# Queries and keys of the fourth retention head: two blocks of eight-step sums replaced by one quad of seven half-token products

## The chip, the cores and the metric

The kernel runs on one core of a Trainium2 chip. The core has a matrix engine (TensorE, shown as PE; its weight loads are shown apart as PEld), three engines for elementwise work (VectorE, DVE; ScalarE, ACT; GpSimd, POOL), a sync engine whose queue issues transfers (SP), and 16 DMA engines that move data between the core's memory SBUF and the outer memory HBM. TensorE writes only to PSUM, a small memory of eight banks, from which the other engines take the sums. The metric is the device time of one execution in microseconds (us). The kernel before takes 1007.98 us, the median of three runs from 1007.86 to 1008.79.

## The reference

One layer of a bidirectional encoder, on 512 tokens of 1024 features, in float32. Cut to what matters here:

```python
h = rmsnorm(x, g_mix)
proj = h @ w_in                # columns: conv x, conv B, conv C, q, k, v, swish gate, gate A, gate R
qf = rotary(q by heads) * (256 ** -0.5)
kf = rotary(k by heads)        # 4 heads of 256 features
def rotary(t):
    t1, t2 = t[..., :128], t[..., 128:]
    return concatenate([t1 * cos - t2 * sin, t1 * sin + t2 * cos])
ret = retention over the tokens, forwards and backwards, of qf, kf, v
y_r = (groupnorm(ret) * g_ret * silu(g_sw)) @ w_r_out
x = x + (sigmoid(gate_a) * y_a + sigmoid(gate_r) * y_r) @ w_o     # y_a: the short convolution
x = x + (silu(h2 @ w_ff_gate) * (h2 @ w_ff_up)) @ w_ff_down
return rmsnorm(x, g_final)
```

The change touches `h @ w_in` for the 256 columns of q and the 256 columns of k of one head, and the rotary turn of these.

## The kernel before

Every float32 operand of a product is written as a sum of two parts in the format that TensorE takes at full rate: `split` (lines 213 to 224) lets ACT make the rounded part (line 216) and DVE the remainder (line 217). A product then takes three matmuls: high by high, high by low, low by high.

Most of the products are done as quads: two groups of weight columns and two halves of the tokens are taken as a two by two block product, with seven block products in place of eight (the Winograd form of Strassen's scheme). The sums of activations are made once (`sums`, line 715). The sums of weights are made as the weights are used: `prefetch_form` (line 311) adds two tiles of 128 by 1024 on DVE (line 322) for the forms t1 to t4, and splits the outcome into a pair of tiles whi and wlo from a pool of five pairs. The forms come in the order b11, t1, t2, b21, t3, t4, b22. A tile pair is called a unit here.

There are two ways to do a quad. `strassen` (line 469) gives sums with the tokens in the partitions. Its units serve 12 matmuls of 512 columns each, a form has two units, and a quad has 14 units and 168 matmuls. `fm_quad` (line 418) gives sums with the features in the partitions. A form is one unit there, and serves 24 matmuls of 256 columns (`prod`, line 407); a quad has 7 units and 168 matmuls. It keeps three banks: a and d are each added into several times, b once. Between the products ACT copies the sums so far out of bank a (`snap`, line 464: p1, u2 and u3), and DVE makes the four outcomes, each a tile of 128 by 512: the two halves of its columns are the two blocks of 128 features, at 256 tokens. They are handed to four functions: ev11 (after the fourth product), ev22 (after the fifth), ev21 (after the sixth; it gets bank a itself) and ev12 (after the seventh).

The third way, `feature_major` (line 383), does without sums of weights. It takes a block of 256 weight columns, two units in all, and for each of the two groups of 128 features it adds up eight steps of three matmuls of 512 columns (`mm3`, line 373). `do_qk` uses it twice for the fourth head, once for q and once for k.

The turn of q and k is `rotate` (line 755): for each of two outcomes, two multiplications by the tables of cosine and sine and one addition or subtraction on DVE, then `keep` (line 664), which splits the outcome (one ACT cast, one DVE subtraction) and stores both parts in HBM through the POOL queue. Each of these uses four tiles t of 128 by 512 (a, b, and the two parts), from a pool of nine that all snaps and sums use as well. The first three heads (EARLY = 3) have their sums early, and are turned later, one turn (of q or of k) behind each of the quads that follow (`turn_one`, line 770, called at ev21 of `do_quad`).

The main part runs in this order: sums of q and k of the first three heads; four quads of v and the swish gate (called v0 to v3 below), the fourth followed by `do_qk(3)`; two quads of the gates A and R (g0, g1); then `mix_quads` (line 887) with three `fm_quad` (x0, x1, x2) for the convolution; then retention and the rest. Loads of weights are listed in `plan` and `loads`, and go through the SP queue up to four entries of the plan ahead (LEAD), into ten raw tiles. Units are prepared at least two ahead (AHEAD). A planner sets the order of the instructions on each engine before the launch, from the order of the program, from which tiles are free, and from its own costs. On the chip each engine takes its instructions in that fixed order.

The names used for units below: g0.4 is the fifth unit of quad g0, counted from 0.

Of the kernel before, what the change touches and what calls it, by code (L numbers as in the profile page):

```python
# [13 lines left out]
F32R = mybir.dt.float32r  # L14
# [5 lines left out]
S = 512  # L20
# [3 lines left out]
QK = 256  # L24
# [5 lines left out]
C_XC, C_GB, C_GC, C_Q, C_K, C_V, C_G, C_GA, C_GR = (  # L30
    0, 1024, 2048, 3072, 4096, 5120, 7168, 9216, 10240)
# [24 lines left out]
FORMS = ("b11", "t1", "t2", "b21", "t3", "t4", "b22")  # L56
# [7 lines left out]
def plan():  # L64

    out = []

    def a(name, col):
        out.append(("c", name, 0, 8, col, 256))

    def b(name, row, nk, col, nc):
        out.append(("c", name, row, nk, col, nc))

    def quad(c0, c1):
        for name in FORMS:  # L80
            for u in (0, 2):
                out.append(("q", ("w", c0, c1), name, u, 2))

    for h in range(EARLY):
        for r in (0, 512):
            b("w_in", r, 4, (C_Q + h * QK, C_K + h * QK), 512)
    for h in range(HEADS):
        quad(C_V + h * VD, C_G + h * VD)
        if h >= EARLY:
            a("w_in", C_Q + h * QK)  # L90
            a("w_in", C_K + h * QK)
    for c in (0, 512):
        quad(C_GA + c, C_GR + c)
    for c0, c1 in ((C_XC, C_GC), (C_XC + 256, C_GC + 256), (C_GB, C_GB + 256)):
        for name in FORMS:
            out.append(("q", ("x", c0, c1), name, 0, 4))
    for s in (2, 3):
        for c in (C_XC, C_GC, C_GB):
            a("w_in", c + s * 256)
    def r(*names):  # L100
        for name in names:
            for u in (0, 2):
                out.append(("q", ("r",), name, u, 2))

    r("b11", "b21")
    out.extend(("q", ("p", 2, c), "b11", u, 2) for c in (0, 1) for u in (0, 2))
    r("t1", "t2", "t3", "b22")
    out.extend(("q", ("p", 3, 1), "b11", u, 2) for u in (0, 2))
    r("t4")
    out.extend(("q", ("p", 3, 0), "b11", u, 2) for u in (0, 2))  # L110
    for kind, name in [("a", x) for x in FORMS[:6]] + [("o", "b11"), ("a", "b22")] + [
            ("o", x) for x in ("t1", "t2", "b21", "b22", "t3", "t4")]:
        for u in (0, 2):
            out.append(("q", (kind,), name, u, 2))
    def f(q, *names):
        for n in names:
            if q == LONE:
                out.append(("q", ("f", q), n, 0, 4))
            else:
                for u in (0, 2):  # L120
                    out.append(("q", ("g", q), n, u, 2))

    def d(q0, n):
        names = FORMS if q0 + n == NQ else EARLY_FORMS
        units = [(name, u) for name in names for u in range(0, n, 2)]
        if q0 + n == NQ:

            i = units.index(("b21", 2))
            units[i:i + 3] = units[i + 1:i + 3] + units[i:i + 1]
        for name, u in units:  # L130
            out.append(("q", ("d", q0), name, u, min(2, n - u)))

    f(0, "b11", "b21")
    f(1, "b11")
    f(0, "t2", "t1", "t3", "t4", "b22")
    f(1, "t1", "t2", "b21", "t3", "t4", "b22")
    f(2, *FORMS)
    d(*FF_PARTS[0])
    f(3, *FORMS)
    f(4, *FORMS)  # L140
    d(*FF_PARTS[1])
    f(LONE, *FORMS)
    d(*FF_PARTS[2])
    return out
# [39 lines left out]
def block_kernel(ctx: ExitStack, tc: tile.TileContext, xw0, xw, xT, xtok, wpack, wquad, cols, decs, gret_rows, rot, g_ffn, g_final, out):  # L184
# [18 lines left out]
    def t512(dt=F32):  # L203
        return tmp.tile([P, 512], dt, tag="t512", name="t512")
# [178 lines left out]
    def feature_major(rhs, evict, block0=0):  # L383

        c = Chunk()
        for m in range(2):
            ps = bank()
            for k in range(8):
                mm3(ps, c.w(k, m * P, P), act_pair(rhs, k), k == 0, k == 7)
            evict(block0 + m, ps)  # L390
# [27 lines left out]
    def fm_quad(forms, ev11, ev21, ev22, ev12):  # L418

        def w():  # L420
            return take()[1][0]
        a, d, b = bank(), bank(), bank()
        prod(w(), forms["a11"], a, True)
        p1 = snap(a)
        prod(w(), forms["s1"], d, True)
        prod(w(), forms["s2"], a, False)
        u2 = snap(a)
        prod(w(), forms["a12"], b, True)
        nc.vector.tensor_tensor(out=p1, in0=b, in1=p1, op=ALU.add)
        ev11(p1)  # L430
        prod(w(), forms["s3"], a, False)
        u3 = snap(a)
        nc.vector.tensor_tensor(out=u3, in0=d, in1=u3, op=ALU.subtract)
        ev22(u3)
        prod(w(), forms["a22"], a, False)
        ev21(a)
        prod(w(), forms["s4"], d, False)
        nc.vector.tensor_tensor(out=u2, in0=d, in1=u2, op=ALU.subtract)
        ev12(u2)
# [133 lines left out]
    rcs = misctile(D, "rcs").rearrange("p (i n) -> p i n", i=2)  # L573
# [81 lines left out]
    qkd = [(kept(f"qh{h}"), kept(f"ql{h}")) for h in range(HEADS)]  # L655
# [6 lines left out]
          for j, n in enumerate((2, 2, 2, 1))]  # L662

    def keep(dst, src):
        hi, lo = t512(F32R), t512(F32R)
        split(src, hi, lo)
        for d, t in zip(dst, (hi, lo)):
            store(d, t.bitcast(F32))
# [83 lines left out]

    nc.vector.tensor_scalar_mul(lgam[:, 4:8], lgam[:, 4:8], -1.0)

    def rotate(h, j, t1, t2, table):
        cos, sin = table[:, 0, :], table[:, 1, :]
        for i, (c1, c2, op) in enumerate(((cos, sin, ALU.subtract), (sin, cos, ALU.add))):
            a, b = t512(), t512()
            nc.vector.tensor_tensor(out=a, in0=t1, in1=c1, op=ALU.mult)
            nc.vector.tensor_tensor(out=b, in0=t2, in1=c2, op=ALU.mult)  # L760
            nc.vector.tensor_tensor(out=a, in0=a, in1=b, op=op)
            keep([t[:, 2 * j + i, :] for t in qkd[h]], a)


    rcn = misctile(D, "rcn").rearrange("p (i n) -> p i n", i=2)
# [8 lines left out]
            rotate(h, j, early[h][:, 2 * j, :], early[h][:, 2 * j + 1, :], rcn)  # L774

    def do_qk(h):
        for j in range(2):
            pss = []
            feature_major(xg, lambda m, ps: pss.append(ps))
            rotate(h, j, *pss, rcs)  # L780


    def do_quad(left, right, func, func_left=None):
        def ev_sum(dst, o, f):
# [396 lines left out]
    def turn(half, th):  # L1181
        name = f"a{th + 1}{half + 1}"
        if not m32:
            t = [bigtile(), bigtile()]
            for j in range(4):
                m32[f"a{j // 2 + 1}{j % 2 + 1}"] = t[j // 2][:, j % 2 * 2:j % 2 * 2 + 2, :].rearrange(
                    "p a (b c) -> p (a b) c", c=256)
        if name != "a21":
            M[name] = form_tile()
        for tt in range(2):  # L1190
            ps = bank()
            for k in range(4):
                nc.tensor.transpose(ps[:, k * P:(k + 1) * P], sga[half][:, 2 * th + tt, k * P:(k + 1) * P], ident)  # L1193
            ps = ps.rearrange("p (k t) -> p k t", k=4)
            sl = slice(tt * P, (tt + 1) * P)
            if name != "a21":
                split(ps, *(t[:, :, sl] for t in M[name]))
            nc.scalar.copy(m32[name][:, :, sl], ps)
# [509 lines left out]
```

## Time and profile before

| what | value |
|---|---|
| median of three runs | 1007.98 us |
| the profiled execution | 1007.38 us, its span 1005.6 us |
| granted TensorE clock | 0.998 |
| PE busy | 995.0 us, 99% |
| DVE busy | 879.2 us, 87% |
| ACT busy | 558.0 us, 55% |
| POOL busy | 161.0 us, 16% |
| the chain that ended last | PE 96%, DVE 3% |

The span is the time from the first to the last instruction of the profiled execution; 1.8 us of its own time lie around it. Busy time is time in which an engine has an instruction of the program under way. Groups are listed by line of the code, engine and operation, with out<-in by the names of the tiles and their shapes. A line can be that of a helper: all splits stand at lines 216 and 217. "A <- B" in a list of waits reads: A waited for B.

### The profile page before, as it was taken

The page shows a single profiled execution, that of the slowest core. Times are in us where ns is not written, and L with a number is a line of the kernel's source. Part 1 is how long each engine was busy: PE and PEld are TensorE (multiplying, and loading weights), DVE is VectorE, ACT ScalarE, POOL GpSimd, SP SyncE. Part 2 cuts the span into 40 slices and gives each one's busy share as a digit, 9 for nine tenths or more (in the row PEclk, how much of TensorE's full clock was granted, in tenths as well). Part 3 has the DMA queues.
Part 4 walks back from the last instruction along what each step waited for, and adds up shares of the span by engine and source line. Part 5 has one row for each costly group of instructions (what it writes and reads, how often), then busy time and mean ns, then how long its engine had stood idle before and what let it go on. Part 6 is the DMA issues. An engine that isn't in the chain of part 4 may idle for free.

```text
span 1005.6 us, 13416 instructions
## 1 busy us (share of the span) xinstructions
PE 995.0 (99%) x4722; PEld 833.4 (83%) x4722; DVE 879.2 (87%) x1145; ACT 558.0 (55%) x751; POOL 161.0 (16%) x256
## 2 busy tenths in 40 slices
PE   9999999999999999999999999999999999999996
PEld 7888888888888998888888888888888888888885
DVE  7878888979798888977897797999988996989897
ACT  7547655563666454433455435577665555574665
POOL 0030221222122004122222110011101000003202
PEclk9999999999999999999999999999999999999999
DMA  9625587695767658899799995467677369487943
GB/s 355 198 76 182 185 287 221 206 306 175 228 196 248 218 224 297 323 321 270 210 246 242 407 308 185 134 211 223 167 229 179 115 213 268 107 249 130 272 143 105
DMA packets 65795, 222.70 MB, mean 221 GB/s; under 512 B 10240, under 2 KB 10368, under 8 KB 61632
## 3 DMA queue, kind: packets, MB, share of 16 engines
q1 hardware_dynamic: 46816, 149.46, 43.8%
q0 software_dynamic: 18624, 72.10, 27.2%
q8 instruction: 37, 0.61, 0.3%
q10 hardware_dynamic: 288, 0.29, 0.1%
q14 instruction: 30, 0.25, 0.1%
HBM read 173.83 MB, written 57.41 MB: 230 GB/s over the span
## 4 chain that ended last, share of the span: by engine, by line
PE 96%; DVE 3%; issue 0%; ACT 0%; POOL 0%; POOLq 0%; DVEq 0%; ACTq 0%
PE bank L459 61%; PE bank L415 8%; PE bank L375 7%; PE bank L376 7%; PE bank L377 7%; PE bank L401 4%; DVE wlo L217 1%; DVE raw L322 0%; PE bank L515 0%; PE bank L1247 0%; PE bank L1193 0%; DVE big L1550 0%; PE bank L700 0%; DVE big L1573 0%; DVE big L217 0%
## 5 line engine op out<-in xcount | busy, mean ns | idle before, releaser
L216 ACT CAST whi<-raw 128x1024 fp32r<-128x1024 f32 (+2 forms) x305 | 308.2, 1029 | 217.3 <-PE bank L459 77.9
L217 DVE TENSOR_TENSOR wlo<-raw,whi 128x1024 fp32r<-128x1024 f32 (+2 forms) x306 | 358.7, 1193 | 76.6 <-ACT whi L216 76.2
L459 PE MATMUL bank<-whi,xform 128*128 128x512 f32 x1056 | 330.5, 390 | 0.0
L459 PEld LDWEIGHTS bank<-whi,xform 128*128 128x128 f32 x1056 | 198.0, 188 | 42.2 <-DVE xform L217 1.1
L459 PE MATMUL bank<-whi,big 128*128 128x512 f32 x708 | 222.4, 389 | 0.2 <-ACT big L1544 0.2
L459 PE MATMUL bank<-wlo,xform 128*128 128x512 f32 x528 | 205.7, 389 | 0.0
L459 PEld LDWEIGHTS bank<-whi,big 128*128 128x128 f32 x708 | 132.9, 188 | 28.5 <-ACT big L1544 0.7
L322 DVE TENSOR_TENSOR raw<-raw 128x1024 f32<-128x1024 f32 x116 | 137.3, 1204 | 0.8
L459 PE MATMUL bank<-wlo,big 128*128 128x512 f32 x354 | 137.9, 390 | 0.0
L459 PEld LDWEIGHTS bank<-wlo,xform 128*128 128x128 f32 x528 | 99.1, 188 | 21.1 <-DVE wlo L217 0.7
L466 ACT COPY t<-bank 128x512 f32<-128x512 f32 x97 | 56.7, 587 | 78.4 <-PE bank L459 61.5
L375 PE MATMUL bank<-big,whi 128*128 128x512 f32 x220 | 85.7, 390 | 0.0
L377 PE MATMUL bank<-big,wlo 128*128 128x512 f32 x220 | 85.6, 389 | 0.0
L376 PE MATMUL bank<-big,whi 128*128 128x512 f32 x220 | 85.6, 389 | 0.0
L459 PEld LDWEIGHTS bank<-wlo,big 128*128 128x128 f32 x354 | 66.5, 188 | 13.9 <-DVE wlo L217 0.3
L415 PE MATMUL bank<-xform,whi 128*128 128x256 f32 x304 | 55.2, 283 | 0.0
L336 POOL DMA_DIRECT2D raw<-wquad x20 | 17.5, 877 | 217.9 <-ACT t L466 66.4
L377 PEld LDWEIGHTS bank<-big,wlo 128*128 128x128 f32 x220 | 41.3, 188 | 8.6
L376 PEld LDWEIGHTS bank<-big,whi 128*128 128x128 f32 x220 | 41.3, 188 | 8.6
L375 PEld LDWEIGHTS bank<-big,whi 128*128 128x128 f32 x220 | 41.3, 188 | 8.5
L415 PEld LDWEIGHTS bank<-xform,whi 128*128 128x128 f32 x304 | 47.5, 192 | 0.3 <-ACT t L466 0.2
L415 PE MATMUL bank<-xform,wlo 128*128 128x256 f32 x152 | 43.0, 283 | 0.0
(218 smaller groups left out, 1300.8 us busy)
## 6 DMA issues: line engine op xcount, KB each, us to landing
raw<-wquad SPq DMA_DIRECT2D x156, 512.0 KB, 5.1
raw<-wpack SPq DMA_DIRECT2D x26, 512.0 KB, 6.0
raw<-wquad POOLq DMA_DIRECT2D x20, 512.0 KB, 6.6
big<-turned SPq DMA_DIRECT2D x112, 64.0 KB, 4.2
t_g<-wquad POOLq DMA_DIRECT2D x12, 512.0 KB, 7.5
z<-t POOLq DMA_DIRECT2D x24, 256.0 KB, 4.6
t_o<-wquad POOLq DMA_DIRECT2D x12, 512.0 KB, 7.8
zform<-z POOLq DMA_DIRECT2D x6, 1024.0 KB, 12.9
```

Source lines behind the costliest of these rows:

```text
L216: first = (round or nc.scalar.copy)(hi, src)
L217: low_of[0] = nc.vector.tensor_tensor(out=lo, in0=src, in1=hi.bitcast(F32), op=ALU.subtract)
L322: nc.vector.tensor_tensor(out=t, in0=t, in1=raws[quad, more, u][:, 0:n], op=ALU.add)
L336: nc.gpsimd.dma_start(out=t[:, 0:n], in_=src[:, 0:n], accum_op=ALU.add)
L375: nc.tensor.matmul(ps, lh, rh, start=first, stop=False)
L376: nc.tensor.matmul(ps, lh, rl, start=False, stop=False)
L377: nc.tensor.matmul(ps, ll, rh, start=False, stop=last)
L401: nc.tensor.matmul(pss[tt], l, r, start=start and kk == 0 and i == 0, stop=stop and kk == 3 and i == 2, skip_group_check=True)
L415: nc.tensor.matmul(o, l[:, c], r[:, k], start=start and s == 0 and k == 0 and i == 0, stop=stop and k == 3 and i == 2, skip_group_check=True)
L459: nc.tensor.matmul(pss[tt], l, r[:, c], start=start and k == 0 and i == 0, stop=stop and k == n - 1 and i == 2, skip_group_check=True)
L466: nc.scalar.copy(t, ps)
```

## The change

The two blocks of q and k of the fourth head are taken out of the list of blocks and put into the plan as seven forms of an `fm_quad`, with q as the first group of columns and k as the second. `do_qk` makes one `fm_quad` in place of two calls of `feature_major`. Its four outcomes are q at the first 256 tokens, q at the last 256, k at the last 256 and k at the first 256; each is turned by itself, with 256 columns of the tables, and stored as half rows. `rotate` and `keep` get a slice of the tokens for this; for the other heads they do as before.

```diff
@@ -87,8 +87,8 @@
     for h in range(HEADS):
         quad(C_V + h * VD, C_G + h * VD)
         if h >= EARLY:
-            a("w_in", C_Q + h * QK)
-            a("w_in", C_K + h * QK)
+            for name in FORMS:
+                out.append(("q", ("x", C_Q + h * QK, C_K + h * QK), name, 0, 4))
     for c in (0, 512):
         quad(C_GA + c, C_GR + c)
@@ -662,7 +662,7 @@
     def keep(dst, src):
-        hi, lo = t512(F32R), t512(F32R)
+        hi, lo = (t512(F32R)[:, 0:src.shape[1]] for _ in range(2))
         split(src, hi, lo)
         for d, t in zip(dst, (hi, lo)):
             store(d, t.bitcast(F32))
@@ -752,14 +752,14 @@
-    def rotate(h, j, t1, t2, table):
-        cos, sin = table[:, 0, :], table[:, 1, :]
+    def rotate(h, j, t1, t2, table, sl=slice(0, S)):
+        cos, sin = table[:, 0, sl], table[:, 1, sl]
         for i, (c1, c2, op) in enumerate(((cos, sin, ALU.subtract), (sin, cos, ALU.add))):
-            a, b = t512(), t512()
+            a, b = (t512()[:, 0:sl.stop - sl.start] for _ in range(2))
             nc.vector.tensor_tensor(out=a, in0=t1, in1=c1, op=ALU.mult)
             nc.vector.tensor_tensor(out=b, in0=t2, in1=c2, op=ALU.mult)
             nc.vector.tensor_tensor(out=a, in0=a, in1=b, op=op)
-            keep([t[:, 2 * j + i, :] for t in qkd[h]], a)
+            keep([t[:, 2 * j + i, sl] for t in qkd[h]], a)
@@ -774,11 +774,9 @@
     def do_qk(h):
-        for j in range(2):
-            pss = []
-            feature_major(xg, lambda m, ps: pss.append(ps))
-            rotate(h, j, *pss, rcs)
-
+        def turn(j, half):
+            return lambda t: rotate(h, j, t[:, 0:256], t[:, 256:512], rcs, slice(256 * half, 256 * half + 256))
+        fm_quad(xf, turn(0, 0), turn(0, 1), turn(1, 1), turn(1, 0))
```

## The prediction

> **What bounds the kernel now.** I read the page's busy times first, then the chain of waits, then the busy time of each engine in the stretches around the change, and last the order of the instructions on DVE, ACT and PE there.
>
> ```profile
> span 1005.6 us, 13416 instructions
> ...
> PE 995.0 (99%) x4722; PEld 833.4 (83%) x4722; DVE 879.2 (87%) x1145; ACT 558.0 (55%) x751; POOL 161.0 (16%) x256
> ...
> 72.11 152.52 PE bank L459 x672
> ...
> 246.39 76.21 PE bank L459 x336
> 322.60 55.13 PE bank L415 x456
> ```
>
> The last three rows are from the chain of waits (start, length, what, how many matmuls). PE sets the time without a break from 72 us through the four v quads, the changed stage (224 to 246 us), both gate quads and the three feature-major quads. So each us of PE work taken out is a us of time, and each us that PE has to wait is one too. In 76.21 us 28 units pass, so a unit of a token-major quad lasts 2.722 us.
>
> ```profile
> 224.60:246.40 21.80, 21.80 (x98) 18.06 (x97) 19.61 (x24) 7.21 (x10) 5.17 (x9) 1.00 0.68 202
> 246.40:284.50 38.10, 38.10 (x169) 31.51 (x169) 31.60 (x37) 23.05 (x30) 6.98 (x13) 1.00 0.65 215
> 284.50:293.90 9.40, 9.40 (x44) 7.76 (x43) 9.40 (x13) 6.91 (x10) 3.56 (x6) 1.00 0.67 195
> 293.90:322.40 28.50, 28.50 (x127) 23.63 (x126) 23.85 (x26) 15.80 (x21) 4.70 (x8) 1.00 0.72 231
> 322.40:342.80 20.40, 20.40 (x170) 20.20 (x169) 18.46 (x23) 10.65 (x15) 2.68 (x5) 1.00 0.78 272
> ```
>
> The columns are stretch, length, then busy time of PE, PEld, DVE, ACT and POOL. The engine to watch is DVE: 19.61 of 21.80 us in the changed stage, 31.60 of 38.10 in g0, and all of the 9.40 us at the start of g1. ACT and POOL are far from full. How close DVE is to holding PE up shows in its order:
>
> ```profile
> 277.61 1.22 DVE L217 TENSOR_TENSOR wlo<-raw,whi 128x1024 fp32r<-128x1024 f32 x1
> ...
> 289.29 3.49 DVE L322 TENSOR_TENSOR raw<-raw 128x1024 f32<-128x1024 f32 x3
> 292.69 5.77 DVE L217 TENSOR_TENSOR wlo<-raw,whi 128x1024 fp32r<-128x1024 f32 x5
> ```
>
> The first is unit g1.1, ready at 278.83. PE begins it at 246.23 + 15 x 2.722 = 287.06, so it is 8.2 us early. The first of the five is g1.4, ready at 292.69 + 1.22 = 293.9; PE begins it at 246.23 + 18 x 2.722 = 295.2. One turn of an earlier head and four evictions in between ate all but 1.3 us of that lead. The lead is what hides DVE work.
>
> **The change part by part. PE** goes from 96 matmuls of 512 columns to 168 of 256. Its bounds are rows of this trace:
>
> ```profile
> 224.47 0.39 PE L375 MATMUL bank<-big,whi 128*128 128x512 f32 x1
> ...
> 246.23 0.39 PE L459 MATMUL bank<-whi,big 128*128 128x512 f32 x1
> ...
> 322.44 0.40 PE L415 MATMUL bank<-big,whi 128*128 128x256 f32 x2
> ...
> 342.79 0.40 PE L415 MATMUL bank<-xform,whi 128*128 128x256 f32 x2
> ```
>
> The stage lasts 246.23 - 224.47 = 21.76 us now. The first feature-major quad, with the same seven products of the same tiles of activations, lasts 342.79 - 322.44 = 20.35 us, its short wait for the copy of bank a included. The term is 20.35 - 21.76 = -1.41 us. A matmul falls from 0.2267 to 0.1211 us, more than half, which is why an eighth less arithmetic brings only 6.5%.
>
> The Trainium skill, in "TensorE: Matmul & The Clock Gate", section "Back-to-back issue gap", gives a warm matmul N/2.4 + 2.5 ns: 216 ns at 512 columns and 109 ns at 256. By it the term would be 168 x 0.109 - 96 x 0.216 = -2.4 us, an estimate from that page. The rows, 0.2267 and 0.1211, do not agree with it, and the sum goes by the rows.
>
> **DVE** loses 4 remainders and gets 7, gets 4 sums of weights and 3 sums of outcomes, and turns in 32 instructions of 256 columns rather than 16 of 512.
>
> ```profile
> 284.55 0.69 DVE L759 TENSOR_TENSOR t<-big,rcn 128x512 f32<-128x512 f32 x1
> 285.15 0.69 DVE L760 TENSOR_TENSOR t<-big,rcn 128x512 f32<-128x512 f32 x1
> ...
> 384.55 0.75 DVE L217 TENSOR_TENSOR t<-big,t 128x256 fp32r<-128x256 f32 x2
> ...
> L217 DVE TENSOR_TENSOR t<-big,t 128x256 fp32r<-128x256 f32 x12 | 4.9, 420 | 0.9 <-ACT t L216 0.9
> ```
>
> From start to start: 1024 columns, (5.77 - 1.22)/4 = 1.14 us; 512 columns, 285.15 - 284.55 = 0.60; 256 columns, 0.75 - 0.42 = 0.33. So the weights cost 3 x 1.14 + 4 x 1.14 = 8.0 us more, the outcomes 3 x 0.60 = 1.8, the turns 32 x 0.33 - 16 x 0.60 = 1.0. DVE gets 10.8 us more work while its stage becomes 1.4 us shorter: 12.2 us of cover are wanted. From 224.6 to 293.9, up to the unit that has the least lead, DVE is idle 2.19 + 6.50 + 0.00 = 8.7 us, and 1.3 us of lead are left: 10.0 us. A first figure for the wait of PE is 12.2 - 10.0 = 2.2 us, if no idle moment is lost and nothing is put off.
>
> A second figure comes from the place where it bites. The new quad begins behind a turn, as x0 does, so I lay x0's order over it, shifted by 322.44 - 224.47 = 97.97 us.
>
> ```profile
> 332.96 2.36 DVE L217 TENSOR_TENSOR wlo<-raw,whi 128x1024 fp32r<-128x1024 f32 x2 [0.21 <-ACT whi L216]
> 335.24 0.68 DVE L429 TENSOR_TENSOR t<-bank,t 128x512 f32<-128x512 f32 x1
> ...
> 254.96 0.69 DVE L217 TENSOR_TENSOR t<-t,t 128x512 fp32r<-128x512 f32 x1
> ...
> 253.98 0.62 ACT L216 CAST t<-t 128x512 fp32r<-128x512 f32 x1 [1.06 <-DVE t L761]
> ...
> 255.54 1.07 ACT L466 COPY t<-bank 128x512 f32<-128x512 f32 x2
> ```
>
> The second of the two units in the first row is the first of the quad that follows, so g0.0 is split at 335.32 - 97.97 = 237.35. The first outcome is made at 335.24 - 97.97 = 237.27, and DVE is free for the turns at 237.87. Quad g0 now starts at 224.47 + 20.35 = 244.82, and g0.4 is wanted at 244.82 + 4 x 2.722 = 255.70. Till then DVE has the four turns, 10.6; two more outcomes, 1.2; g0.1, 1.14; g0.2 to g0.4 with a sum each, 6.8: together 19.7, ready at 257.6, or 1.9 us late. The last remainder of a turn (0.33) can follow, which leaves 1.6. The same product adds into bank a, so both copies of p1 must be done as well; in the last three rows (DVE, then ACT) they run right behind the last cast and remainder of the turn, at 255.54, where g0.4 was wanted at 246.23 + 10.89 = 257.1. They have 0.5 us to spare now. If g0.4's pair comes last on DVE, the turns are over at 257.6 - 0.33 - 2.28 = 255.0, and cast and copies end at 255.0 + 0.40 + 1.07 = 256.5, before g0.4 itself. So I don't count them again.
>
> Idle time of DVE inside the turns comes on top:
>
> ```profile
> DVE wlo L217 <- ACT whi L216: 10.6, 10, 2.2
> DVE t L760 <- DMA v<-t: 2.8, 1, 2.8
> DVE t L217 <- ACT t L216: 0.7, 1, 0.7
> ...
> L216 ACT CAST t<-big 128x256 fp32r<-128x256 f32 x12 | 4.7, 404 | 7.4 <-DVE big L876 6.2 <-DMA z<-t 1.2
> ```
>
> The first three are DVE's waits from 224 to 323 us. The first of them is DVE being far ahead. The third is the round trip to ACT, 0.7 us over four outcomes of turns; for eight with a shorter cast (0.40 us against 0.62) I take 0.7 x 2 x 0.65 = 0.9 us, between 0 and 0.7 + 2.8 = 3.5 twice over, 7. **PE waits 1.6 + 0.9 = 2.5 us**, near the 2.2 of the first figure.
>
> After this place a unit costs DVE at most 2.28 of 2.72 us, and from g0.5 to g0.13 it needs 5 x 2.28 + 4 x 1.14 + 4 x 0.60 = 18.4 of 24.5 us: the lead comes back to about 6 us, and the low point at g1.4 loses some 1 to 2 us of its 1.3. That could cost up to 0.9 us; I take none, as g0's sums may move too.
>
> **ACT, POOL, SP.** ACT gets 3 casts of 1024, 3 copies, and 8 short casts for 4 long, about 3 x 1.03 + 3 x 0.59 + 0.7 = 5.6 us beside 7.21 in a stage of 21.8: hidden. The weights are still four loads of 512 KB on SP, issued up to four entries of the plan ahead rather than with the block: nothing. The stores become 16 of 128 KB for 8 of 256 KB.
>
> ```profile
> qh<-t POOLq DMA_DIRECT2D x16, 256.0 KB, 3.2
> ...
> z<-t POOLq DMA_DIRECT2D x8, 128.0 KB, 4.5
> ...
> L671 POOL DMA_DIRECT2D qh<-t x16: 539/542/566, 110.2 to 326.0; - x16
> ```
>
> A half store lands no sooner than a whole one by these medians (4.5 against 3.2 us), and issuing eight more takes POOL 8 x 0.54 = 4.3 us, where it works 5.17 of 21.80. Queued behind them are only g0's stores and the copies of later weight sums. That is nothing by itself, but each store holds a tile t till it lands, and that is the second rival.
>
> **The sum.** 1005.6 - 1.41 + 2.5 = 1006.7 us of span, 1.1 us over before; laid on the median, **1009.1 us**. A difference under 0.2%, 2 us, is about what a measurement of this kernel can't tell from no change.
>
> **Rivals.**
>
> *All hidden.* The planner spreads the turns of q and k beyond g0.4, as it let them run till 255 us before, and copies p1 ahead of them. For it: units in g0 were still 6.5 us early then; g0.5 was ready at 252.09 + 1.22 = 253.3, and wanted at 246.23 + 5 x 2.722 = 259.8.
>
> ```profile
> 252.09 1.22 DVE L217 TENSOR_TENSOR wlo<-raw,whi 128x1024 fp32r<-128x1024 f32 x1
> ```
>
> Against it: the 12.2 us wanted and 10.0 found. Then the saving stands whole: 1007.98 - 1.4 = 1006.6.
>
> *The tiles t run out* (the other side). Nine tiles serve all; the quad holds p1 and u2 over several products, u3, and four for each of eight outcomes. Before, an outcome took 254.96 + 0.69 - 250.89 = 4.8 us from its first multiplication:
>
> ```profile
> 250.89 0.69 DVE L759 TENSOR_TENSOR t<-bank,rcs 128x512 f32<-128x512 f32 x1
> ```
>
> 2.4 us of that was its own DVE work (4 x 0.60). If the other 2.4 stay, an outcome takes 2.4 + 1.33 = 3.7 us, and eight from 237.87 end at 267.5; six end at 260.1. The copies of p1 follow behind, by two outcomes at the earliest, as each of these holds four of nine tiles. So PE waits from 260.1 + 1.1 - 255.7 = 5.5 up to 267.5 + 1.1 - 255.7 = 12.9 us. It decides from a wait of 3.4 us on, where the saving is gone and 2 us more. I price it near the lower end, as the units put between are counted with the outcomes, at 6: 1007.98 - 1.4 + 6 = 1012.6. Against it: half as long an outcome leaves less for others to be put between. The Trainium skill, in "Perfetto Trace Analysis", section "Identifying Performance Opportunities", says that gaps that recur on the engine that should be full can mean too few buffers for the next tile; no run here shows such gaps yet.
>
> *PE saves more.* If the narrow matmul took half of the wide one, 0.1134, the quad would take 19.0 us and the change 2.7 us less: 1005.3. This is the direction of the first rule of the skill. Row 322.44 to 342.79 speaks against it.
>
> **How the numbers follow.** Forecast (a wait of PE from 0.7 to 3.4 us, time from 1007.3 to 1010.0): 0.45. All hidden: 0.17. Tiles run out: 0.32. PE saves more, or the planner's new order frees time elsewhere: 0.06. Same: 0.45 + 0.17 less 0.05 at the edges, of which 0.04 are slower and 0.01 faster. The predicted time is 1009.1. The range goes from 1006.4, just under all hidden, to 1013.5, past the price of the second rival; under 2 in 10 is left out. The forecast's own range is 1007.3 to 1010.0. Faster 0.07, same 0.57, slower 0.36.
>
> **What would show it.** The seven products without waits last 20.2 to 20.4 us. DVE busy over the new quad and g0 rises by about 11 us, and runs without a gap from the first turn to g0.4. PE's first gap stands at g0.3 to g0.5 or, under the second rival, at the copies of p1 or u3, with the releaser an ACT copy of line 466 rather than a remainder of line 217. I am wrong if PE waits at another place, such as in the quad itself for u3, if the lead at g1.4 is gone, or if the end of the kernel moves by more than the stage does.

## The result and the profile after

The changed kernel takes 1019.0 us, the median of four runs (1018.75 to 1019.43); beside it the kernel before took 1008.38 us (1007.86 to 1008.8). The ratio is 1.0106, with a 95% interval from 1.0088 to 1.0124: slower by 1.1%, some 10.6 us, where 1.1 us was forecast. The profiled execution took 1019.43 us, 12.1 us of span more than before.

The page of the changed kernel, its busy times and two rows of its 40 slices (25.4 us each):

```profile
span 1017.7 us, 13618 instructions
...
PE 996.5 (98%) x4794; PEld 837.4 (82%) x4794; DVE 889.5 (87%) x1171; ACT 561.8 (55%) x761; POOL 165.2 (16%) x264
...
PE   9999999999599999999999999999999999999996
...
PEclk9999999999799999999999999999999999999998
```

DVE works 889.5 - 879.2 = 10.3 us more, close to the 10.8 of the prediction. PE is busy in every slice but the eleventh, 254 to 280 us, and in that same slice its clock drops. So the whole loss stands at one place. The chain of waits shows which:

```profile
265.84 5.14 DMA ql<-t
271.00 0.59 ACT t L466
271.63 62.87 PE bank L459 x264
334.50 55.15 PE bank L415 x456
```

Quad x0 starts at 334.50 instead of 322.60, 11.90 us later; almost the whole difference of the spans is there by then. PE resumes at 271.63, released by an ACT copy of line 466: a copy of p1 of quad g0. PE itself, in time:

```profile
224.67 0.40 PE L415 MATMUL bank<-big,whi 128*128 128x256 f32 x2
...
239.06 0.40 PE L459 MATMUL bank<-whi,big 128*128 128x512 f32 x1
...
247.93 0.40 PE L415 MATMUL bank<-big,whi 128*128 128x256 f32 x2
...
253.68 0.40 PE L459 MATMUL bank<-whi,xform 128*128 128x512 f32 x1
...
255.75 0.39 PE L459 MATMUL bank<-whi,big 128*128 128x512 f32 x1
...
260.96 0.39 PE L459 MATMUL bank<-whi,big 128*128 128x512 f32 x1
271.63 0.79 PE L459 MATMUL bank<-whi,xform 128*128 128x512 f32 x1 [10.28 <-ACT t L466]
...
277.65 0.62 PE L459 MATMUL bank<-whi,xform 128*128 128x512 f32 x2
```

The new quad begins at 224.67. After five of its products PE starts g0, at 239.06, and comes back for the last two from 247.93 to 253.68: 14.39 + 5.75 = 20.14 us for the seven products. At 255.75 it takes g0's product a12, which adds into other banks and which the planner has moved ahead of the one that needs p1 out of bank a. That fills 5.4 us; then PE is idle for 10.28 us. From start to start it is 271.63 - 260.96 = 10.67 us, of which one matmul's pitch, 0.23, is no loss: 10.44 us. From 271.63 to 277.65 only some 14 matmuls begin, 0.427 us apart instead of 0.227: another 14 x 0.20 = 2.8 us. The granted clock shows why. The columns are stretch, length, busy time of PE, PEld, DVE, ACT and POOL, then granted clock, DMA share and GB/s:

```profile
246.00:262.00 16.00, 15.35 (x91) 13.34 (x89) 16.00 (x26) 8.31 (x11) 3.78 (x7) 1.00 0.15 53
...
262.00:271.60 9.60, 0.00 (x0) 0.00 (x0) 8.70 (x18) 2.86 (x6) 3.11 (x6) 0.60 0.86 274
...
264.30:277.90 13.60, 6.26 (x16) 4.93 (x17) 7.69 (x16) 6.36 (x10) 4.81 (x9) 0.52 0.94 311
277.90:284.00 6.10, 6.10 (x28) 5.04 (x27) 2.51 (x3) 3.47 (x5) 0.00 (x0) 1.00 0.26 86
```

The clock fell to half during the gap and stayed there until 6 us after PE had work again. DVE is busy for all of the first stretch and for 8.70 of the 9.60 us of the second, in which PE stands still; most of its idle time in the third comes after the turns. So its busy time alone doesn't tell whether DVE has too much to do or does things in the wrong order. Its order shows what it did with its time:

```profile
239.20 0.42 DVE L759 TENSOR_TENSOR t<-t,rcs 128x256 f32<-128x256 f32 x1
...
239.87 1.22 DVE L322 TENSOR_TENSOR raw<-raw 128x1024 f32<-128x1024 f32 x1
241.01 0.42 DVE L761 TENSOR_TENSOR t<-t,t 128x256 f32<-128x256 f32 x1
...
242.48 1.22 DVE L217 TENSOR_TENSOR wlo<-raw,whi 128x1024 fp32r<-128x1024 f32 x1
243.61 0.42 DVE L217 TENSOR_TENSOR t<-t,t 128x256 fp32r<-128x256 f32 x1
...
249.30 1.21 DVE L217 TENSOR_TENSOR wlo<-raw,whi 128x1024 fp32r<-128x1024 f32 x1
...
270.80 0.43 DVE L217 TENSOR_TENSOR t<-t,t 128x256 fp32r<-128x256 f32 x1 [0.49 <-ACT t L216]
```

This is the first outcome of the turn: between its multiplication and its addition stands a sum of weights, and before its remainder a remainder of weights. So it goes on, with 15 such instructions inside the eight outcomes and two between them: the outcomes last from 239.20 to 270.80 + 0.43, four us each on average, of which 4 x 0.33 = 1.3 are their own. Most of the units in between are early. The row at 249.30 is the remainder of g0.4, ready at 250.51 and used by PE at 271.63. What PE waits for comes at the end of the row of outcomes, on ACT:

```profile
270.37 0.41 ACT L216 CAST t<-t 128x256 fp32r<-128x256 f32 x1 [2.20 <-DVE u L822]
...
271.00 1.07 ACT L466 COPY t<-bank 128x512 f32<-128x512 f32 x2 [0.23 <-DMA ql<-t]
```

The two copies of p1 stand directly behind the last cast of the turn (before the change the cast of a unit stood between); the last 0.23 us they wait for a tile t that a store still holds. So the place is that of the second rival, the tiles t. The experiments ask what exactly holds the copies back.

### The profile page after: what moved, and what is told of

The parts are those of the page before. It is cut to its first block, busy times and chain, and to the rows that moved or that the text cites. A ratio compares the mean times of both kernels' runs of the same rounds, so it can differ in the third digit from the quotient of the medians.

```text
span 1017.7 us, 13618 instructions
## 1 busy us (share of the span) xinstructions
PE 996.5 (98%) x4794; PEld 837.4 (82%) x4794; DVE 889.5 (87%) x1171; ACT 561.8 (55%) x761; POOL 165.2 (16%) x264
## 4 chain that ended last, share of the span: by engine, by line
PE 90%; issue 4%; DVE 3%; POOL 1%; DMA 1%; ACT 0%; POOLq 0%; DVEq 0%; ACTq 0%
PE bank L459 58%; PE bank L415 8%; PE bank L375 6%; PE bank L376 6%; PE bank L377 6%; PE bank L401 4%; DVE wlo L217 1%; DMA ql<-t 1%; DVE raw L322 0%; POOL qh L671 0%; DMA first<-xw 0%; POOL ql L671 0%; PE bank L1245 0%; PE bank L1191 0%; DVE big L1548 0%
## 5 line engine op out<-in xcount | busy, mean ns | idle before, releaser
L459 PE MATMUL bank<-whi,xform 128*128 128x512 f32 x1056 | 332.6, 392 | 10.3 <-ACT t L466 10.3
L322 DVE TENSOR_TENSOR raw<-raw 128x1024 f32<-128x1024 f32 x120 | 141.7, 1200 | 3.3 <-DMA raw<-wquad 2.6
L375 PE MATMUL bank<-big,whi 128*128 128x512 f32 x188 | 73.3, 390 | 0.0
L377 PE MATMUL bank<-big,wlo 128*128 128x512 f32 x188 | 73.2, 389 | 0.0
L376 PE MATMUL bank<-big,whi 128*128 128x512 f32 x188 | 73.1, 389 | 0.0
L415 PE MATMUL bank<-xform,whi 128*128 128x256 f32 x368 | 66.8, 283 | 0.0
L415 PEld LDWEIGHTS bank<-xform,whi 128*128 128x128 f32 x368 | 57.5, 192 | 0.3 <-ACT t L466 0.2
L415 PE MATMUL bank<-xform,wlo 128*128 128x256 f32 x184 | 52.1, 283 | 0.0
L375 PEld LDWEIGHTS bank<-big,whi 128*128 128x128 f32 x188 | 35.3, 188 | 7.4
L377 PEld LDWEIGHTS bank<-big,wlo 128*128 128x128 f32 x188 | 35.3, 188 | 7.4
L376 PEld LDWEIGHTS bank<-big,whi 128*128 128x128 f32 x188 | 35.3, 188 | 7.3
```

The costliest lines, as they stand in the source:

```text
L322: nc.vector.tensor_tensor(out=t, in0=t, in1=raws[quad, more, u][:, 0:n], op=ALU.add)
L375: nc.tensor.matmul(ps, lh, rh, start=first, stop=False)
L376: nc.tensor.matmul(ps, lh, rl, start=False, stop=False)
L377: nc.tensor.matmul(ps, ll, rh, start=False, stop=last)
L415: nc.tensor.matmul(o, l[:, c], r[:, k], start=start and s == 0 and k == 0 and i == 0, stop=stop and k == 3 and i == 2, skip_group_check=True)
L459: nc.tensor.matmul(pss[tt], l, r[:, c], start=start and k == 0 and i == 0, stop=stop and k == n - 1 and i == 2, skip_group_check=True)
```

## The experiments

Three theories had to be told apart. T: nine tiles t are too few, because an outcome holds four of them. F: the tiles of one pool are handed out in the order of the program, so that p1's copies cannot come before the last outcome, however many are free. D: DVE has too much to do. F was put forward after e1, e2, e6 and e9, whose expectations know only T and D; the runs from e10 on test it. In each kernel below the time of the kernel before was taken on the same chip. "Idle" is the time of PE in brackets in a row; the loss is 0.16 us more, since a matmul of 512 columns ends 0.39 us after it began and the next could begin after 0.23.

### e1_packed: half as many tiles per outcome

```diff
     def keep(dst, src):
-        hi, lo = (t512(F32R)[:, 0:src.shape[1]] for _ in range(2))
+        hi, lo = (lambda t: (t[:, 0:256], t[:, 256:512]))(t512(F32R)) if src.shape[1] == 256 else (t512(F32R), t512(F32R))
...
-            a, b = (t512()[:, 0:sl.stop - sl.start] for _ in range(2))
+            a, b = (lambda t: (t[:, 0:256], t[:, 256:512]))(t512()) if sl.stop - sl.start == 256 else (t512(), t512())
```

> Edit: in the turns by halves, a and b share one tile t of 512 columns, and so do the two parts, so that an outcome takes two tiles of the nine rather than four; the work of every engine is the same. Theory T (the copies of p1 of quad g0 wait for a free tile t, which the eight outcomes hold): the gap of PE ahead of the third product of g0 falls from 10.4 us to under 4, the clock is not halved, time 1007 to 1011. Theory D (DVE has more work than time, whatever the tiles): the same DVE work, the gap stays at 8 us or more, time 1016 to 1020.

Measured: 1018.23 us (1017.82 to 1019.06) against 1008.42, ratio 1.0099 (1.0082 to 1.0116). First PE, then ACT:

```profile
270.53 0.80 PE L459 MATMUL bank<-whi,xform 128*128 128x512 f32 x1 [7.49 <-ACT t L466]
```

```profile
269.60 0.40 ACT L216 CAST t<-t 128x256 fp32r<-128x256 f32 x1
269.90 1.06 ACT L466 COPY t<-bank 128x512 f32<-128x512 f32 x2
```

An outcome takes two tiles instead of four, and the copies still come directly behind the last cast: 269.90 - 225.26 = 44.6 us after the quad's first matmul, where the changed kernel has 271.00 - 224.67 = 46.3. The idle time is 7.49 us where T expected less than 4, and the time lies in D's range. The number of tiles is not the cause: T falls.

### e2_no_sums: the quad without its sums of weights

```diff
-        if more and not joined(quad, f):
+        if more and not joined(quad, f) and quad != ("x", C_Q + EARLY * QK, C_K + EARLY * QK):
```

> Edit: the four sums of weights of the new quad are left out (t1 to t4 are then b11, b11, b12, b11 alone, and q and k of the fourth head come out otherwise), so DVE has 4 x 1.14 = 4.6 us less to do; the tiles t are used as before. Theory T: the gap stays at 8 to 11 us, time 1015 to 1019. Theory D: the gap is 4.6 us shorter or more, 6 us at most, time 1013 or less.

The four sums of weights of the new quad are left out (4.6 us of DVE by the row of 1.14), and q and k of the fourth head are other numbers. Measured: 1018.78 us in one run, against 1008.42.

```profile
269.81 0.80 PE L459 MATMUL bank<-whi,xform 128*128 128x512 f32 x1 [8.09 <-ACT t L466]
```

The quad began at 224.91 here, so PE resumed 44.9 us after it rather than 47.0. Taking 4.6 us of work from DVE brought that 2.1 us forward, and left an idle time of 8.09 us, with the same releaser. That speaks against D, but doesn't settle it: the sums left out stand ahead of the turns, and DVE then sat idle there for 1.60 and 1.65 us, so only a part of the 4.6 us was taken from what delays the copies. The runs e6 and e12, in which DVE has the work of the change, decide it.

### e6_p1_big: p1 of g0 into a tile of another pool

```diff
-        p1 = [snap(x) for x in a]
+        p1 = p1(a) if p1 else [snap(x) for x in a]
...
+    def in_big(a):
+        t = bigtile()
+        for tt in range(2):
+            nc.scalar.copy(t[:, tt, :], a[tt])
+        return [t[:, 0, :], t[:, 1, :]]
...
-        do_quad(gad[j], grd[j], AF.Sigmoid, AF.Sigmoid)
+        do_quad(gad[j], grd[j], AF.Sigmoid, AF.Sigmoid, None if j else in_big)
```

> Edit: the two copies of p1 of quad g0 go to a tile of the pool of big tiles, not to two tiles t; nothing else changes. Theory T: the copies run as soon as the first product of g0 is over, and the gap at the third product is gone; the next to want tiles t, the copies of u2, may wait instead, for what is left of the turns, so a gap of 0 to 5 us at the fifth product; time 1007 to 1013. Theory D: units or outcomes are late all the same, time 1015 or more.

Measured: 1014.43 us in one run, against 1008.42. PE, then ACT:

```profile
272.83 0.79 PE L459 MATMUL bank<-whi,xform 128*128 128x512 f32 x1 [6.14 <-ACT t L466]
```

```profile
271.89 0.40 ACT L216 CAST t<-t 128x256 fp32r<-128x256 f32 x1
272.20 1.06 ACT L466 COPY t<-bank 128x512 f32<-128x512 f32 x2
```

p1's copies were in time, and PE went through the products s2 and a12. It then stopped at the next copies that take tiles t, those of u2, and these again stand directly behind the last cast of the turn. The idle time and the total lie just above what was expected (0 to 5 us, up to 1013). With the same work for DVE the wait moved to the next copies that share the pool with the outcomes and come later in the program. This is what F says.

### e9_half_turns: the blocks of before, turned by halves

```diff
             feature_major(xg, lambda m, ps: pss.append(ps))
-            rotate(h, j, *pss, rcs)
+            for sl in (slice(0, 256), slice(256, 512)):
+                rotate(h, j, pss[0][:, sl], pss[1][:, sl], rcs, sl)
```

This is an edit of the kernel before; `keep` and `rotate` take a slice as in the change.

> Edit: the kernel before, with its two blocks of eight steps, but each of the two turns made in two halves of the tokens (eight outcomes of 256 columns with four tiles t each, 16 stores of half rows). Theory T (outcomes hold tiles for their round trips, not for their DVE work): a gap at the copies of p1 of g0, 3 to 8 us, time 1011 to 1017. Theory D: 1.0 us more DVE work, covered by the 8.7 us of idle time: time within 1 us of before, no gap.

Measured: 1013.86 us in one run, against 1008.42. PE, ACT, and the stretch with the lowered clock:

```profile
266.18 0.50 PE L459 MATMUL bank<-whi,xform 128*128 128x512 f32 x1 [2.16 <-ACT t L466]
```

```profile
265.23 0.41 ACT L216 CAST t<-t 128x256 fp32r<-128x256 f32 x1
265.54 1.07 ACT L466 COPY t<-bank 128x512 f32<-128x512 f32 x2
```

```profile
266.90:270.40 3.50, 3.50 (x11) 2.71 (x10) 1.05 (x2) 2.16 (x3) 2.10 (x4) 0.52 0.95 282
```

Without the quad, turning by halves alone moves the copies of p1 from 31.1 us after the start of the stage (255.54 - 224.47) to 39.8 (265.54 - 225.77) and costs 5.4 us, more than the quad can save. The idle time, 2.16 us, is a little less than T's 3 to 8, and the time is far from D's. Its eight outcomes have 17 instructions for units between their own, where the four whole ones of the kernel before have 11: fewer for each outcome, but more in all.

The change delays the copies further, to 46.3 us. The rest comes from the quad itself: its first outcome can be turned 239.20 - 224.67 = 14.5 us after its start, while the kernel before makes the first multiplication of its turns after 232.53 - 224.47 = 8.1:

```profile
232.53 0.68 DVE L759 TENSOR_TENSOR t<-bank,rcs 128x512 f32<-128x512 f32 x1
```

So of the 46.3 - 31.1 = 15.2 us, about 9 come with the halves and about 6 with the later first outcome.

### e7_no_turn: the quad alone

```diff
         def turn(j, half):
-            return lambda t: rotate(h, j, t[:, 0:256], t[:, 256:512], rcs, slice(256 * half, 256 * half + 256))
+            return lambda t: None
...
-        return [load(t, F32R) for t in qkd[h]], tab
+        return [load(t, F32R) for t in qkd[min(h, EARLY - 1)]], tab
```

> Edit: the quad of q and k as changed, but its four outcomes are not turned and not stored (the scores of the fourth head are made from the third head's q and k instead). What is left is the products and the 8.0 + 1.8 us of DVE work for weights and outcomes. All theories: PE goes without a gap through g0 if the turns are the cause; the stage and g0 together shrink by 1.41 us against before, time 1006.4 to 1007.2. If the weights' sums alone hold PE up, a gap of 1 us or more stands in g0.

The fourth head isn't turned and not stored; the third head's q and k stand in for it. Measured: 1006.25 us in one run, against 1008.12, just under the range expected.

```profile
246.00:284.00 38.00, 38.00 (x169) 31.46 (x168) 30.24 (x33) 22.80 (x28) 5.41 (x10) 1.00 0.56 187
```

PE has no gap. From the quad's first matmul to x0's first it is 96.37 us (224.23 to 320.60) against 97.97 before: the quad saves 1.60 us by itself. The loss of the changed kernel between the same two points closes with it: 334.34 - 224.67 = 109.67, or 11.70 more than before, and -1.60 + 10.44 + 2.8 = 11.6.

### e10_gather: outcomes copied to a large tile and turned as whole rows

```diff
-        fm_quad(xf, turn(0, 0), turn(0, 1), turn(1, 1), turn(1, 0))
+        t = bigtile()
+        def put(j, half):
+            def ev(x, out=t[:, 2 * j:2 * j + 2, 256 * half:256 * half + 256]):
+                nc.scalar.copy(out, x.rearrange("p (m t) -> p m t", m=2))
+            return ev
+        fm_quad(xf, put(0, 0), put(0, 1), put(1, 1), put(1, 0))
+        for j in range(2):
+            rotate(h, j, t[:, 2 * j, :], t[:, 2 * j + 1, :], rcs)
```

> Edit: the four outcomes of the quad are first copied by ACT into one big tile, and then turned at once as whole rows of 512 tokens, four outcomes of four tiles t rather than eight. Theory F (the tiles of one pool are handed out in the order of the program, so g0's copies of p1 come behind the last outcome of the turns, and each outcome of the turns takes its own DVE time and two instructions of 1.14 us for the units that DVE does in between): four outcomes of 4.7 us from about 242.5 end at 261 to 262, just when the products that can be moved ahead are used up; gap 0 to 3 us, time 1006.5 to 1010. Theory D: about the work of the change with 1 us less on DVE; gap within 2 us of the change's 10.4.

Measured: 1011.46 us in one run, against 1008.12.

```profile
258.92 0.50 PE L459 MATMUL bank<-wlo,big 128*128 128x512 f32 x1 [1.60 <-DVE wlo L217]
...
265.66 0.50 PE L459 MATMUL bank<-whi,xform 128*128 128x512 f32 x1 [1.42 <-ACT t L466]
```

```profile
258.00:270.00 12.00, 9.66 (x41) 7.65 (x42) 12.00 (x15) 6.10 (x10) 2.88 (x6) 1.00 0.48 169
```

With four outcomes instead of eight the wait for p1 is 1.42 us rather than 10.28, as F expected (0 to 3), though the time is above its 1006.5 to 1010. The wait isn't nothing, as all four now start behind the quad. Before it stands a wait for a unit, with DVE busy for all of the 12 us. From the quad to x0 it is 100.05 us, 2.1 more than before; the other 1.2 us of this single time lie behind x0 and were not followed.

### e11_held: the same, turned behind g1

```diff
-            rotate(h, j, early[h][:, 2 * j, :], early[h][:, 2 * j + 1, :], rcn)
+            rotate(h, j, early[h][:, 2 * j, :], early[h][:, 2 * j + 1, :], rcn if h < EARLY else rcs)
...
+        early.append(t)
+        held.extend((h, j) for j in range(2))
```

These lines stand on top of the copies of e10, whose two turns are left out.

> Edit: the four outcomes of the quad are copied by ACT into one big tile, which joins the sums of the first three heads; the two turns are made later, as whole rows, behind the quads that follow and after g1, by the order that the held turns have. Theory F: g0's copies of p1 have no turn in front of them but the usual one, so no gap; PE keeps the 1.41 us, time 1006.6 to 1007.6, 0.08 to 0.18% under before, unless the two turns after g1 hold up the copies of x0 (then up to 4 us more). Theory D: the DVE work is the same in sum, spread over more time; 1007 to 1010.

Measured: 1021.52 us (1020.85 to 1021.77) against 1008.12, ratio 1.0131 (1.0114 to 1.0147).

```profile
336.44 0.80 PE L415 MATMUL bank<-big,whi 128*128 128x256 f32 x2 [5.33 <-ACT whi L216]
...
339.97 0.58 PE L415 MATMUL bank<-big,wlo 128*128 128x256 f32 x1 [2.73 <-DVE wlo L217]
```

The expectation missed. g0 and g1 ran without a gap, and x0 began 96.36 us after the quad, with the saving whole. Then x0 lost it all and more: three turns now stand directly ahead of it, and its units came late, with waits of 5.33 and 2.73 us, three of about 1 us or less, and the clock at half for 13.65 us in all. Here DVE is short, in a quad whose units serve 24 matmuls of 0.12 us.

### e12_turn_big: turns by halves with tiles of the other pool

```diff
+        n = sl.stop - sl.start
+        own = bigtile(F32R).rearrange("p a b -> p (a b)") if n < S else None
...
-            a, b = (t512()[:, 0:sl.stop - sl.start] for _ in range(2))
+            if own is None:
+                a, b, hi, lo = t512(), t512(), t512(F32R), t512(F32R)
+            else:
+                a, b, hi, lo = (own[:, (4 * i + k) * n:(4 * i + k + 1) * n] for k in range(4))
+                a, b = a.bitcast(F32), b.bitcast(F32)
...
```

> Edit: the turns by halves take their four tiles per outcome from the pool of big tiles (one big tile holds the two outcomes of a turn by halves), not from the nine tiles t; work and stores are the same. Theory F: the copies of p1 are no longer behind the turns, the gap of 10 us ahead of g0's third product is gone. In the order that the planner then sets the turns come in one go ahead of the units of g0, so PE may wait for units instead, 2 to 5 us, with a remainder of line 217 as its releaser; time 1008 to 1012. Were the number of tiles or DVE's time the cause, the gap at the copies of line 466 would stay.

Measured: 1011.3 us in one run, against 1008.12. Two stretches, then PE:

```profile
239.00:253.00 14.00, 12.03 (x76) 10.30 (x74) 14.00 (x37) 5.96 (x12) 7.57 (x14) 1.00 0.53 196
...
254.00:258.00 4.00, 3.41 (x9) 2.75 (x10) 4.00 (x5) 1.25 (x2) 0.23 (x1) 0.57 0.18 66
```

```profile
252.39 0.73 PE L459 MATMUL bank<-whi,xform 128*128 128x512 f32 x2 [1.98 <-ACT whi L216]
...
254.59 0.80 PE L459 MATMUL bank<-wlo,xform 128*128 128x512 f32 x1 [1.47 <-DVE wlo L217]
```

The complement of e6: now the outcomes leave the pool, and the copies of p1 come at 249.09 and 250.50. The wait for them is gone. All eight outcomes are turned in one go in 14 us, in which DVE is never idle, and PE then waits for unit g0.2, 3.8 us from start to start beyond the pitch. This is a shortage of DVE like the one that was forecast, two units ahead of g0.4, where it was forecast; it comes into sight once the copies are out of the way.

### e14_big_no_sums: e12 without the sums of weights

The edits of e12 and of e2 together; q and k of the fourth head are other numbers, as in e2.

> Edit: the turns take their tiles from the big pool, as in the run before with that edit, and the four sums of weights of the new quad are left out besides (q and k of the fourth head come out otherwise). If what is left of the wait there (2.36 + 1.86 us between matmuls at g0's second product, for units) is DVE's lack of time, then 4.6 us less work, of which 2.3 us can be used ahead of the turns for sums of g0, shortens it by 2 us or more, and the halved clock behind it goes: time 1008.5 to 1010 from 1011.3. If it is the order alone, the wait stays within 0.5 us of 3.8 and the time at 1011 or more.

Measured: 1008.24 us in one run, against 1008.27. PE's waits up to x0:

```profile
253.13 0.73 PE L459 MATMUL bank<-whi,xform 128*128 128x512 f32 x2 [0.48 <-ACT whi L216]
...
254.60 0.50 PE L459 MATMUL bank<-whi,xform 128*128 128x512 f32 x1 [0.74 <-ACT whi L216]
...
261.42 0.50 PE L459 MATMUL bank<-wlo,xform 128*128 128x512 f32 x1 [0.59 <-DVE wlo L217]
```

The same 4.6 us of DVE work that made little difference in e2 take PE's idle time at this place from 3.45 to 0.48 + 0.74 = 1.22 us, with 0.59 us more at 261.42, and the half clock is gone. So what is left in e12 is DVE's time, and in the changed kernel that shortage is covered by the other wait.

### e13_k_later: q at once, k behind g0's fourth product, both with tiles of the other pool

```diff
+        def put(half):
+            return lambda t: nc.scalar.copy(k[:, :, 256 * half:256 * half + 256], t.rearrange("p (m t) -> p m t", m=2))
+        fm_quad(xf, turn(0), turn(1), put(1), put(0))
+        later.append(lambda: rotate(h, 1, k[:, 0, :], k[:, 1, :], rcs, far=True))
...
+                    if later and dst is left:
+                        later.pop()()
```

`turn` and `rotate` take the large tiles as in e12; k is a large tile of its own, and is turned as whole rows.

> Edit: the quad as changed; q is turned by halves at once, with tiles from the big pool; the two outcomes of k are copied by ACT into a big tile and turned as whole rows after the fourth product of g0, with tiles from the big pool too. So no turn of this head stands in the queue for the tiles t, and DVE has 5 us less to do between 238 and 256 us. Theory F with the shortage of DVE as the next limit: DVE then needs 14.4 of the 17.8 us up to g0.4, and the rest falls where it was idle 6.5 us in g0; no gap of PE over 1 us from the quad to the end of g1; the 1.4 to 1.6 us that the quad saves stay: 1006.4 to 1007.2, 0.10 to 0.16% under before. If the tiles were not the matter, or DVE has no room in g0, a gap of 2 us or more in g0 or at the start of g1, 1008.5 or more.

Measured: 1007.1 us (1006.21 to 1007.38, 11 runs) against 1008.27 (15 runs), ratio 0.9986 with an interval from 0.9977 to 0.9995. PE's only wait of note up to x0, and the stretch that answers to e7's:

```profile
298.35 0.50 PE L459 MATMUL bank<-wlo,xform 128*128 128x512 f32 x1 [0.27 <-DVE wlo L217]
```

```profile
246.00:284.00 38.00, 38.00 (x171) 31.51 (x170) 37.18 (x45) 24.83 (x33) 8.88 (x17) 1.00 0.57 195
```

From the quad to x0 it is 96.94 us (225.12 to 322.06), 1.03 less than before. DVE does the work of the turns between units that are early enough, 37.18 of 38.0 us, and PE isn't held up. So the change can bring its saving, or two thirds of it, if the turns use other tiles than the copies between products and half of them are put off by 20 us. It is a little faster than the kernel before, by 0.14%, and the only kernel here with the whole work that gains.

## Why the prediction was wrong

**The term of PE** was right: -1.41 us forecast, -1.60 measured in e7, and 20.14 - 21.76 = -1.62 in the changed kernel itself. The rows of this kernel were the better guide than the figure of the Trainium skill ("TensorE: Matmul & The Clock Gate", section "Back-to-back issue gap") that the prediction set against them, which the page gives for an isolated matmul and by which it would have been -2.4.

**DVE's work** was right too, 10.8 us forecast and 10.3 measured. That it can make PE wait for units of g0 was right as a mechanism, with 2.5 us forecast for g0.4 and 3.8 measured at g0.2 in e12, in another order of the work. But in the changed kernel this wait doesn't show, since g0.4 is ready 21 us before PE uses it.

**The step that failed** is the sentence "If g0.4's pair comes last on DVE, the turns are over at 255.0, and cast and copies end at 256.5, before g0.4 itself. So I don't count them again." The copies of p1 ended at 271.00 + 1.07 = 272.1. I had supposed that the turns run together and the units follow by need. The planner does the opposite: in each outcome some two instructions of 1.14 us for units go between the instructions that wait for one another, whether PE needs these units soon or not. So units are early and the turn is late, and whatever stands behind the turn is later still. The row that says so was in the prediction: 4.8 us for an outcome, of which 2.4 its own. 2.4 + 2 x 1.14 = 4.7 before the change, 1.33 + 2 x 1.14 = 3.6 after it: halving an outcome halves its own part, but hardly lessens what is put between. In all, 17 such instructions stand in the row of eight outcomes, where the row of four had 11; with the two evictions that now fall into it, it lasts 270.80 + 0.43 - 239.20 = 32.0 us instead of 254.96 + 0.69 - 232.53 = 23.1. I used the length of an outcome for the rival and not for the forecast's own order.

**The rival "the tiles t run out"** had the place (g0's copies of p1), the releaser (an ACT copy of line 466) and the length of an outcome (3.7 us forecast, 4.0 measured on average). Three things in it were off. Its price, 6 us of wait, was taken near the lower of its ends, 5.5 to 12.9, with the reason that the units put between are counted with the outcomes. That gave no ground for the lower end. And the argument against the rival, that a shorter outcome leaves less to be put between, held for one outcome but not for the row. By the upper end the time would have been 1007.98 - 1.4 + 12.9 = 1019.5, which is close to the measured 1019.0, partly by chance: the turns ended later than its 267.5, at 271.2; against that the planner filled 5.4 us with a12, which I had not foreseen; and the half clock added 2.8. Its cause was given as the number of tiles, and e1 shows that this is not it: half the tiles per outcome leave the copies where they are. The shared pool is the cause (e6 moves the wait to the next copies, e12 removes it, each by taking one side to another pool), and a handing out in the order of the program is the reading that fits all three; it was inferred from the order of instructions and not seen directly. And its chance, 0.32, was below that of a forecast which rested on an order of instructions that no row showed.

**The range** ended at 1013.5, just past the price of that rival, and not at its upper end, though both ends had been worked out.

**The rival "all hidden"** is nearly what e13 does: 1007.1 against the 1006.6 of that rival, with other tiles and with k put off. The planner didn't come to it by itself.

**The low point in g1**, for which I had allowed up to 0.9 us and taken none, cost nothing in the changed kernel, where DVE gained the time in which PE stood still. (Two readings of the prediction were off, without bearing on the sum: two evictions of DVE, not four, stand ahead of g1.4, and before the change the cast of a unit stands between the last cast of the turn and the copies of p1.) In e13, which has no such gift, a wait stands in g1 at 298.35, of 0.27 + 0.16 = 0.43 us.

What stays open: why the outcomes in e1 still take about 4 us each though they hold few tiles, while in e12, with tiles of their own pool, they run in one go. Whether the stores prolong the row of outcomes was not tried by itself; the chain shows one of 5.14 us just ahead of the copies, but these come only 0.23 us later for it than the last cast allowed, and e12 makes the same stores.

## What to carry to other kernels

An operation cut into halves brings about half of its own work each, but the waits between its instructions come once for each half, and here the planner put more into them in all (17 instructions for 11); so cost a turn by what one takes in the trace from first to last instruction, and then ask what stands behind it. Look for the small copies that share a pool of tiles with such a row of work and come later in the program: two copies, 1 us in all, came 16 us late here (272.1 for 255.7), and moving the turns to another pool took this wait away, where halving the number of tiles did not; moving the copies only handed the wait on to the next ones. When both ends of a cost are worked out and differ by 7 us, the range must hold the end that nothing in the profile excludes.

## What the chip showed beside this

An idle PE costs more than its idle time, because the granted clock falls to half and stays there for some us after the work is back. In the changed kernel it was at half for 13.65 us, beginning inside the idle time of 10.28 us and ending 5.9 us after it. In the other kernels such stretches lasted 10.24 us (idle 7.49 in e1 and 8.09 in e2), 6.83 (6.14 in e6) and 3.41 (2.16 in e9; 1.98 and 1.47 close together in e12); e11, with several gaps in x0, has one of 10.24 and one of 3.41. All are multiples of 3.41 us. Idle times of 1.60 and 1.42 us in e10, 6.7 us apart, had none, and neither had the waits of e14 and e13. The Trainium skill, in "TensorE: Matmul & The Clock Gate", section "What's actually happening", describes a clock with the two states full and half, decided in windows of 3413 ns that run freely; the lengths agree, and so does the 0.52 in the rows, whose stretches reach a little beyond the half clock. In "HAM oscillation — how this bites in real kernels" the page puts the rule as no idle gaps of PE above about 3.4 us. Here 2.16 us were enough, and the measurement decides: a gap need not be as long as a window to cost one.

By the rows of the changed kernel, a window at half clock in which PE has work costs an estimated 3.41 x (0.427 - 0.227)/0.427 = 1.6 us. So the wait that the chain shows is not the whole price of a gap.
